# Output projection of the hyena group for all tokens at once, with twice-used weights split once and kept on chip

## The chip, the cores and the metric

The kernel runs on one core of a Trainium2 chip. The metric is device time in microseconds (us) of one execution, the median of several runs. Engines are named as in the profile: PE is TensorE (matrix products), PEld its weight loads, DVE VectorE, ACT ScalarE, POOL GpSimd and SP SyncE, which issues the loads from HBM.

## What is computed

One layer of a diffusion trunk with 512 latent tokens and 256 context tokens, model width 1024, all in float32. Cut to what matters here:

```python
# first half-step SwiGLU, then one input projection p_lat = u_lat @ w_in[layer]
y_lat = jnp.concatenate([hyena_mixer(p_lat[..., :hy_end], *hyena_params),                  # 512 channels
                         diff_head_out(o_lat, diff_subln_g[layer], lam_init)], axis=-1)    # 512 channels
h_lat = h_lat + mod_lat[5] * (y_lat @ w_out[layer])
h_lat = ffn_half_step(h_lat, norm_g[layer, 2], mod_lat[6], mod_lat[7], mod_lat[8], *ffn1)  # RMSNorm, then SwiGLU
return rms_norm(h_lat, final_g)
```

`w_out` is 1024 x 1024. Its first 512 rows meet the hyena group's output (group 0 in the kernel), its last 512 rows the output of the four attention heads (group 1).

## The kernel before

Tokens lie along the free dimension, channels along the 128 partitions. Every float32 operand of a product is split into a high part `h` (a cast to fp32r on ACT, line 253) and a low part `l` (a subtraction on DVE or on POOL, line 254). `mm3` then makes three products from one tile of weights and one of tokens: high by high (line 268), high by low (269), low by high (270).

`stream` brings weights: it loads 1 MB from HBM into one of two raw buffers (line 259) and splits it in two pieces of 128x1024, so one call costs two casts on ACT and two subtractions on DVE or POOL. Without `blocks` the pieces go into rings of three high and three low buffers (`r_h`, `r_l`), where a new piece waits until PE has read the one three pieces back.

Work of this part of the kernel is cut into generators, and the string `SCHEDULE` lists which generator goes on by one step at which place. A `g` behind a word gives the subtractions of that step to POOL, a `v` gives POOL's other elementwise work to DVE. The Tile framework then places the instructions on the engines in about that order; a later, ready instruction may be put ahead of an earlier one that it expects to wait. On the chip every engine runs its own list in order.

The words that the change and the prediction touch:

- `s`, `w`, `a` and `n` with a head and a query block or a half: scores (lines 1196 and 1197, softmax 1199 to 1203), weights of the difference (1213 to 1216), attention (transposes at 1228, products, copy at 1240) and the norm of a head (1254 to 1262). Halves 0 and 1 are tokens 0 to 255 (`SEG_A`) and 256 to 511 (`SEG_B`).
- `J` loads and splits the hyena output. `H0` and `H1` multiply it by group 0 of `w_out`, one half of the tokens each (`wo(0, half)`); `W0` and `W1` do so for the attention output and group 1 (`wo(1, half)`). Each has eight steps, one for every 128 output channels: twelve products of 256 columns and one evacuation (`wo_evac`, line 1269) that adds the result to the residual stream. Each of the four streams `w_out` of its group anew, in two calls of `stream`, at its first and its fifth step.
- `N0` and `N1` are the RMSNorm of a half after the projection: squares on ACT (386, 389), their sum on DVE (391), a product with `ones_d` on PE (399), the inverse root (366 to 369), then eight steps of scaling with a split (407 to 413).
- `F` is the first part of the second SwiGLU, for `N_FIRST` = 2 tiles of hidden channels and each half of the tokens: tiles 0 and 1 of half A, then 0 and 1 of half B. Each has 48 products of 256 columns and streams its weights anew. What the schedule leaves of `F` runs in `plain2`, before the rest of the SwiGLU starts.

`N0` needs the evacuations of `H0` and `W0`, and `N1` those of `H1` and `W1`. In the schedule before, `H0` lies among scores, attention and head norms; `W0` follows it; six of the eight steps of `H1` come between `W0` and the end of `N0`'s scaling, the other two shortly after it.

The on-chip buffers of fp32r words lie at hand-chosen places: the stacked queries and keys of head 3 at 14336 to 18432, the split hyena output at 22528 to 26624, both of `F`'s halves in rings, and the three extra weight buffers of the second SwiGLU (`x`) at 27648, 34880 and 35904.

## Time and profile before

| | us |
|---|---|
| three runs, median (lowest, highest) | 1323.02 (1321.09, 1324.64) |
| the profiled execution, time | 1323.46 |
| the profiled execution, span of its instructions | 1321.7 |
| busy in the span: PE | 1240.0 (94%) |
| DVE | 1088.6 (82%) |
| ACT | 571.0 (43%) |
| POOL | 141.6 (11%) |
| DMA | mean 112 GB/s, 147.82 MB |

A product's duration in the trace runs from its issue to the end of its flow through the array, so that neighbours overlap: for the rate of PE one reads the distance of two starts. A bracket at the end of a row gives the time for which the engine was idle before the instruction, and what ended it. PEclk is the granted clock as a share of 2.4 GHz; 0.50 is 1.2 GHz. The projection and what stands around it take the stretch from about 833 to 976 us of the span.

### The profile page before, as it was taken

What the parts mean: (1) busy time and instruction counts of PE and PEld (TensorE: products, weight loads), DVE (VectorE), ACT (ScalarE), POOL (GpSimd) and SP (SyncE); (2) the same over time, 40 slices, a digit from 0 to 9 for tenths busy, and PEclk for the clock granted to TensorE, in tenths of its full rate; (3) what the DMA queues carried; (4) which work ended last, traced back from release to release, by engine and by line L of the source; (5) the groups of instructions that cost most, each with busy time, mean ns of one, the idle gap of its engine ahead of it and who ended that gap; (6) DMA issues with size and microseconds to landing.
All of it is one profiled execution on the core that took longest, in us unless ns stands there. A gap on an engine that the chain in (4) does not pass through costs nothing.

```text
span 1321.7 us, 19654 instructions
## 1 busy us (share of the span) xinstructions
PE 1240.0 (94%) x7722; PEld 1129.2 (85%) x7722; DVE 1088.6 (82%) x1751; ACT 571.0 (43%) x980; POOL 141.6 (11%) x134
## 2 busy tenths in 40 slices
PE   5899899999999999999989999887899999999996
PEld 2479799999998999999878998776787989989895
DVE  6988899999998765678789667888898978879776
ACT  5652334222331432444343457685553534535343
POOL 3640000000000000000225022113110000000001
PEclk9899999999999999999989999999999999999998
DMA  7646304454573221221323112202342222323221
GB/s 278 218 135 220 114 32 134 154 174 159 176 246 120 84 76 64 80 80 65 109 82 112 49 49 70 75 33 96 128 144 80 98 95 96 123 96 102 96 65 64
DMA packets 30828, 147.82 MB, mean 112 GB/s; under 512 B 3536, under 2 KB 3920, under 8 KB 21648
## 3 DMA queue, kind: packets, MB, share of 16 engines
q1 hardware_dynamic: 28880, 140.28, 31.8%
q0 software_dynamic: 1856, 6.29, 1.3%
q8 instruction: 60, 0.98, 0.3%
q14 instruction: 32, 0.26, 0.1%
HBM read 141.32 MB, written 5.24 MB: 111 GB/s over the span
## 4 chain that ended last, share of the span: by engine, by line
PE 69%; DVE 16%; ACT 4%; DMA 3%; POOL 3%; issue 2%; DVEq 0%; ACTq 0%; POOLq 0%; SPq 0%
PE dc L702 19%; PE ab L702 13%; PE dn L269 6%; PE dn L270 6%; PE dn L268 6%; DVE arena_r L254 3%; ACT arena_r L253 1%; DVE arena_f L353 1%; DVE arena_f L391 1%; DMA arena_f<-in_ada 1%; DMA arena_f<-in_wd 1%; PE gu L269 1%; PE gu L270 1%; DVE arena_f L1199 1%; PE gu L268 1%
## 5 line engine op out<-in xcount | busy, mean ns | idle before, releaser
L680 ACT CAST arena_r<-arena_f 128x512 fp32r<-128x512 f32 x340 | 210.1, 622 | 435.5 <-PE dn L269 167.9
L685 DVE TENSOR_TENSOR arena_r<-arena_f,arena_r 128x512 fp32r<-128x512 f32 x340 | 233.3, 692 | 46.4 <-ACT arena_r L680 40.1
L702 PE MATMUL dc<-arena_r 128*128 128x384 f32 (+1 forms) x1272 | 197.6, 309 | 1.6 <-DVE arena_f L728 1.5
L702 PEld LDWEIGHTS dc<-arena_r 128*128 128x128 f32 x1272 | 188.8, 190 | 2.4 <-DVE arena_f L728 2.1
L253 ACT CAST arena_r<-arena_f 128x1024 fp32r<-128x1024 f32 (+3 forms) x159 | 128.8, 829 | 141.4 <-DVE arena_f L1050 29.1
L254 DVE TENSOR_TENSOR arena_r<-arena_f,arena_r 128x1024 fp32r<-128x1024 f32 (+3 forms) x145 | 144.0, 1009 | 26.7 <-ACT arena_r L253 24.5
L702 PE MATMUL ab<-arena_r 128*128 128x384 f32 (+1 forms) x1008 | 159.3, 309 | 3.0 <-DVE arena_f L921 3.0
L702 PEld LDWEIGHTS ab<-arena_r 128*128 128x128 f32 x1008 | 150.9, 190 | 3.7 <-issue 1.8
L269 PE MATMUL dn<-arena_r,arena_r 128*128 128x512 f32 (+1 forms) x420 | 146.1, 348 | 1.3 <-DVE arena_r L254 1.2
L268 PE MATMUL dn<-arena_r,arena_r 128*128 128x512 f32 (+1 forms) x420 | 145.3, 347 | 1.6 <-ACT arena_r L253 1.6
L270 PE MATMUL dn<-arena_r,arena_r 128*128 128x512 f32 (+1 forms) x420 | 145.2, 346 | 0.0
L754 DVE SCALAR_TENSOR_TENSOR arena_f<-dn,hg,arena_f 128x512 f32<-128x512 f32 (+1 forms) x136 | 83.9, 638 | 47.5 <-PE dn L270 46.9
L673 DVE TENSOR_TENSOR arena_f<-arena_f 128x512 f32<-128x512 f32 x144 | 98.7, 687 | 4.3 <-DMA arena_f<-in_wgu 2.7
L268 PEld LDWEIGHTS dn<-arena_r,arena_r 128*128 128x128 f32 x420 | 79.4, 189 | 12.6 <-ACT arena_r L253 2.5
L269 PEld LDWEIGHTS dn<-arena_r,arena_r 128*128 128x128 f32 x420 | 79.5, 189 | 12.3 <-DVE arena_r L254 2.6
L353 DVE SCALAR_TENSOR_TENSOR arena_f<-arena_f,cs 128x1024 f32<-128x1024 f32 x70 | 88.5, 1280 | 1.6 <-DMA arena_f<-in_ada 1.4
L254 POOL TENSOR_TENSOR arena_r<-arena_f,arena_r 128x1024 fp32r<-128x1024 f32 (+1 forms) x14 | 30.9, 2211 | 544.5 <-DVE arena_f L726 444.2
L270 PEld LDWEIGHTS dn<-arena_r,arena_r 128*128 128x128 f32 x420 | 79.4, 189 | 9.7
L702 PE MATMUL dc<-arena_r,arena_r 128*128 128x384 f32 (+1 forms) x456 | 72.5, 310 | 0.0
L702 PEld LDWEIGHTS dc<-arena_r,arena_r 128*128 128x128 f32 x456 | 68.0, 190 | 0.6
L702 PE MATMUL ab<-arena_r,arena_r 128*128 128x384 f32 (+1 forms) x288 | 47.3, 309 | 0.0
L702 PEld LDWEIGHTS ab<-arena_r,arena_r 128*128 128x128 f32 x288 | 43.6, 190 | 0.0
(306 smaller groups left out, 2604.4 us busy)
## 6 DMA issues: line engine op xcount, KB each, us to landing
arena_f<-in_wgu SPq DMA_DIRECT2D x46, 1024.0 KB, 4.9
arena_f<-in_ada SPq DMA_DIRECT2D x62, 512.0 KB, 3.8
arena_f<-in_wd SPq DMA_DIRECT2D x44, 512.0 KB, 3.6
arena_f<-in_win SPq DMA_DIRECT2D x10, 1024.0 KB, 4.8
arena_f<-in_wout SPq DMA_DIRECT2D x8, 1024.0 KB, 4.8
arena_e<-in_ada SPq DMA_DIRECT2D x10, 512.0 KB, 6.4
arena_f<-in_xT SPq DMA_DIRECT2D x2, 1024.0 KB, 7.3
arena_f<-in_dft SPq DMA_DIRECT2D x2, 1024.0 KB, 4.9
```

Of the source, the lines that this page charges most:

```text
L253: S.copy(hi, src)
L254: eng.tensor_tensor(out=lo, in0=src, in1=hi.bitcast(F32), op=ALU.subtract)
L268: T.matmul(out_, lh, rh, start=start, stop=False)
L269: T.matmul(out_, lh, rl, start=False, stop=False)
L270: T.matmul(out_, ll, rh, start=False, stop=stop)
L353: V.scalar_tensor_tensor(out=acc, in0=w, scalar=sc, in1=acc, op0=ALU.mult, op1=ALU.add)
L391: eng.tensor_tensor(out=acc_b.v(n), in0=acc_b.v(n), in1=sq[k % 2].v(n), op=ALU.add)
L673: V.tensor_tensor(out=o, in0=p, in1=q, op=op)
L680: S.copy(slots[i % NS][0][:, :src.shape[1]], src)
L685: V.tensor_tensor(out=l, in0=src, in1=h.bitcast(F32), op=ALU.subtract)
L702: T.matmul(o, w[:, k, :], b[:, k, :], start=j < 4 and k + n == 0, stop=k == 3 and n == 2, skip_group_check=True)
L754: V.scalar_tensor_tensor(out=dst, in0=t, scalar=hg[:, seg[2], idx, d:d + 1], in1=dst, op0=ALU.mult, op1=ALU.add)
```

## The change

Three places where weights were loaded and split twice are changed.

- `H0` and `H1` become one part `H`, which multiplies the hyena output for all 512 tokens: eight steps of twelve products of 512 columns and one evacuation of 512 columns. Group 0 of `w_out` is streamed in two calls where there were four. In the schedule all steps of `H` stand before `W0`: two among the scores of heads 2 and 3 where four of `H0` stood, and six between `w23` and the second step of `s33`.
- `W0` streams group 1 of `w_out` into eight blocks of its own (`KEEP_AT`), and `W1` reads them again: two calls where there were four. The first four blocks lie where the stacked queries and keys of head 3 are, the other four where the split hyena output is.
- `F` streams its two tiles into eight blocks of its own (`FIRST_AT`) for half A and reads them again for half B: two calls where there were four.

The extra weight buffers `x` of the second SwiGLU move to three of the kept blocks. The words of the schedule other than `H`, `H0` and `H1` keep their order and their suffixes.

```diff
+KEEP = 2
+KEEP_AT = (14336, 15360, 16384, 17408, 22528, 23552, 24576, 25600)
+FIRST_AT = (20480, 21504, 26624, 27648, 32832, 33856, 34880, 35904)
 # SCHEDULE, from the first word that differs (lines wrapped anew)
-Q3g s20 J w20 s21 Q3 K3 a11 H0 a11 s21 w21 a11 K3v s30 s30 s31 H0g s31 a20 a20 w30 H0 a20 s22 H0 s22 w31 a30
-s23 a30 s23 n00g n00 w22 w23 H0 n10 a30 H0g n20g n10g n20 H0 n30 s32 s32 n30 s33 a21 n00g n20 n30g a21 n10 s33
-H0g w32 W0 W0g a21 W0g W0 W0 W0 W0g W0g w33 H1g H1g H1 a31 N0 N0g H1 N0g n01gv a31 a31 N0 H1g H1g N0 n21 N0
-n11 H1 H1g n31 n01 F n21g n11 n31g n31v n01 Fg n11 n21v W1g W1 W1g W1 W1 W1g W1v W1g N1g N1g N1 Fv N1g N1v N1
+Q3g s20 J w20 s21 Q3 K3 a11 H a11 s21 w21 a11 K3v s30 s30 s31 s31 a20 a20 w30 H a20 s22 s22 w31 a30
+s23 a30 s23 n00g n00 w22 w23 H n10 a30 n20g n10g n20 H n30 s32 H s32 H n30 H s33 H a21 n00g n20 n30g a21 n10 s33
+w32 W0 W0g a21 W0g W0 W0 W0 W0g W0g w33 a31 N0 N0g N0g n01gv a31 a31 N0 N0 n21 N0
+n11 n31 n01 F n21g n11 n31g n31v n01 Fg n11 n21v W1g W1 W1g W1 W1 W1g W1v W1g N1g N1g N1 Fv N1g N1v N1
...
     def wo(group, half):
-        seg = (SEG_A, SEG_B)[half]
+        seg = (SEG_A, SEG_B)[half] if group else SEG_L
         if group:
             yh, yl = [b.v(4, 256) for b in yat[half]]
         else:
-            yh, yl = [b.v(4, TL)[:, :, 256 * half:256 * half + 256] for b in late["yhy"]]
+            yh, yl = [b.v(4, TL) for b in late["yhy"]]
         for rw in range(2):
-            res = stream(a["wout"][group, rw])
+            if group:
+                kept = late.setdefault("wkeep", {})
+                if rw not in kept:
+                    blocks = None
+                    if rw < KEEP:
+                        blocks = [R.get(1024, x) for x in KEEP_AT[4 * rw:4 * rw + 4]]
+                        late["wblocks"] = late.get("wblocks", []) + blocks
+                    kept[rw] = stream(a["wout"][group, rw], blocks=blocks)
+                res = kept[rw] if rw < KEEP else kept.pop(rw)
+            else:
+                res = stream(a["wout"][group, rw])
...
-                    t = bank1(f"wo{group}{half}{d}")[:, :256]
+                    t = bank1(f"wo{group}{half}{d}")[:, :seg[1]]
...
     def first_tiles():
+        kept = {}
         for t0, n, _ in (SEG_A, SEG_B):
             for f in range(N_FIRST):
-                wgt = stream(a["wgu"][f])
+                if f not in kept:
+                    blocks = [R.get(1024, x) for x in FIRST_AT[4 * f:4 * f + 4]]
+                    kept[f] = stream(a["wgu"][f], blocks=blocks), blocks
+                wgt = kept[f][0]
...
-               {"x": (A_AT + 9216, R2_AT + 6144, R2_AT + 7168), "act": R2_AT,
+               {"x": (22528, 23552, 24576), "act": R2_AT,
```

## Rows read from the trace of the kernel before

**Rows 1.** The page, part 1 (engine, busy, share, instructions) and part 4 (chain that ended last).

```profile
PE 1240.0 (94%) x7722; PEld 1129.2 (85%) x7722; DVE 1088.6 (82%) x1751; ACT 571.0 (43%) x980; POOL 141.6 (11%) x134
...
PE 69%; DVE 16%; ACT 4%; DMA 3%; POOL 3%; issue 2%; DVEq 0%; ACTq 0%; POOLq 0%; SPq 0%
```

**Rows 2.** Busy time of each engine in six stretches; columns: span, PE, PEld, DVE, ACT, POOL, PEclk, DMA.

```profile
833.00:862.80 29.80, 23.65 (x149) 20.47 (x146) 26.88 (x47) 20.80 (x41) 3.46 (x3) 0.94 0.18 66
862.80:883.50 20.70, 17.82 (x112) 16.02 (x113) 17.06 (x39) 17.26 (x30) 3.62 (x4) 0.92 0.14 44
883.50:898.20 14.70, 14.26 (x114) 13.62 (x113) 13.14 (x22) 10.98 (x23) 3.76 (x3) 1.00 0.25 83
898.20:935.70 37.50, 26.91 (x190) 24.68 (x188) 30.84 (x54) 20.13 (x35) 15.70 (x11) 0.95 0.24 85
935.70:947.60 11.90, 11.76 (x92) 11.20 (x92) 10.97 (x21) 6.00 (x12) 0.00 (x0) 1.00 0.52 178
947.60:976.10 28.50, 21.80 (x147) 20.89 (x147) 21.69 (x38) 15.47 (x24) 4.29 (x4) 0.88 0.32 112
```

**Rows 3.** Instructions on the projection's PSUM tiles: duration min/median/max in ns, first and last start.

```profile
L270 PE MATMUL wo<-arena_r x96: 278/283/415, 835.5 to 947.4; 128*128 128x256 f32 x96
...
L1269 DVE SCALAR_TENSOR_TENSOR arena_f<-wo,mod,arena_f x32: 470/479/487, 837.8 to 947.7; 128x256 f32<-128x256 f32 x32
...
L270 PE MATMUL wo<-arena_r,arena_r x32: 277/283/283, 883.8 to 898.1; 128*128 128x256 f32 x32
```

**Rows 4.** PE in order of time: start, duration; consecutive starts of 256- and 512-column products.

```profile
793.26 0.39 PE L269 MATMUL q_ps<-arena_r 128*128 128x512 f32 x1
...
793.49 0.39 PE L270 MATMUL q_ps<-arena_r 128*128 128x512 f32 x1
...
894.99 0.28 PE L268 MATMUL wo<-arena_r,arena_r 128*128 128x256 f32 x1
...
895.11 0.28 PE L269 MATMUL wo<-arena_r,arena_r 128*128 128x256 f32 x1
```

**Rows 5.** Groups of POOL's instructions, 840 to 985 us: count, busy, mean ns, idle before.

```profile
L254 POOL TENSOR_TENSOR arena_r<-arena_f,arena_r 128x1024 fp32r<-128x1024 f32 x6 | 14.8, 2475 | 13.1 <-ACT arena_r L253 13.1
```

**Rows 6.** DVE in order of time, 899 to 934 us: 128x256 operations and one wait.

```profile
899.09 2.41 DVE L391 TENSOR_TENSOR arena_f<-arena_f 128x256 f32<-128x256 f32 x1 [0.48 <-ACT arena_f L389]
...
902.43 0.42 DVE L391 TENSOR_TENSOR arena_f<-arena_f 128x256 f32<-128x256 f32 x1 [0.54 <-ACT arena_f L389]
...
903.80 2.26 DVE L391 TENSOR_TENSOR arena_f<-arena_f 128x256 f32<-128x256 f32 x1 [0.55 <-ACT arena_f L389]
...
911.30 0.48 DVE L1269 SCALAR_TENSOR_TENSOR arena_f<-wo,mod,arena_f 128x256 f32<-128x256 f32 x1 [2.67 <-PE wo L270]
...
927.74 2.63 DVE L254 TENSOR_TENSOR arena_r<-arena_f,arena_r 128x256 fp32r<-128x256 f32 x1
...
933.55 2.13 DVE L254 TENSOR_TENSOR arena_r<-arena_f,arena_r 128x256 fp32r<-128x256 f32 x1 [0.49 <-ACT arena_r L253]
```

**Rows 7.** PE in order of time, 922 to 964 us: waits, with what ended them.

```profile
922.79 0.48 PE L1256 MATMUL om<-arena_f,ones_e 128*128 128x256 f32 x1 [3.38 <-ACT arena_f L1254]
...
935.74 0.38 PE L269 MATMUL wo<-arena_r 128*128 128x256 f32 x1 [1.78 <-DVE arena_r L254]
...
951.32 0.48 PE L399 MATMUL ms_c<-arena_f,ones_d 128*128 128x256 f32 x1 [3.67 <-DVE arena_f L391]
...
963.38 0.39 PE L269 MATMUL gu<-arena_r 128*128 128x256 f32 x1 [1.92 <-POOL arena_r L413]
```

**Rows 8.** PE in two microseconds after a wait: span, busy, granted clock, DMA.

```profile
952.00:954.00 2.00, 2.00 (x12) 0.50 0.00 0
```

**Rows 9.** Last score product on PE; early split of the first W0 weights on ACT and DVE.

```profile
855.53 1.05 ACT L253 CAST arena_r<-arena_f 128x1024 fp32r<-128x1024 f32 x1
...
878.43 1.22 DVE L254 TENSOR_TENSOR arena_r<-arena_f,arena_r 128x1024 fp32r<-128x1024 f32 x1
...
879.23 0.34 PE L1197 MATMUL sc<-arena_r 128*128 128x384 f32 x1
```

25 lines of the change are left out of this document (14 added, 11 removed).

## The prediction

> **What bounds the kernel now.** I read the page first, then the busy time by stage, then the waits, and last single rows of PE, DVE and POOL around the projection. The page calls PE busy for 94% of the span, but PE carries only 69% of the chain that ended last, and DVE 16% [rows 1]. So there are places where PE waits, and the question is whether the change lies in one of them. The stages say that it does. From 833 to 976.1 us PE is busy for 23.65, 17.82, 14.26, 26.91, 11.76 and 21.80 us of six stretches that last 143.1 us together [rows 2]: 26.9 us are empty, and two thirds of that are in two stretches, the one after `W0` (898.2 to 935.7: 10.6 us empty) and the one after `W1` (947.6 to 976.1: 6.7 us). These are the norms `N0` and `N1`, the scaling and the start of `F`. In the first of them DVE is busy for 30.84 of 37.5 us [rows 2]. Within it I looked at what the long waits of PE end on: an operation of a head norm on ACT (3.38 us), a subtraction on DVE (1.78 us); after `W1` the sum of squares on DVE (3.67 us) and a subtraction on POOL (1.92 us) [rows 7]. Here the vector work sets the pace and PE follows it. `W0` and `W1` themselves are bound by PE: 14.26 of 14.7 us and 11.76 of 11.9 us [rows 2].
>
> **PE's own work: -1.1 us, counted in the stretches below.** A product of 256 columns starts 0.12 us after the one before it, one of 512 columns 0.23 us [rows 4]. The three lines of `mm3` make 3 x (96 + 32) = 384 products for the four old parts [rows 3], that is 96 for each. `H0` and `H1` cost 192 x 0.12 = 23.0 us; `H` costs 96 x 0.23 = 22.1 us. Fewer products are thus no gain by themselves. The evacuations stay about equal: 16 of 0.479 us [rows 3] become 8 that I bound by twice that.
>
> **What moves.** Half of the old work, `H1`, stood after `W0`: 96 x 0.12 = 11.5 us of PE. It now stands ahead of `W0`. I sum by stretch.
>
> *833 to 862.8, no change.* Four old steps (4 x 12 x 0.12 = 5.8 us) give way to two new ones (2 x 12 x 0.23 = 5.5 us).
>
> *862.8 to 883.5, +6.9 us.* Four old steps (5.8 us) give way to six new ones (72 x 0.23 = 16.6 us): 10.8 us more on PE. The stretch has 20.7 - 17.82 = 2.9 us without PE work, and its granted clock is 0.92 [rows 2], so about 0.08 x 20.7 = 1.7 us of full speed are lost. New products can fill at most these 4.6 us, at least nothing: +6.2 to +10.8 us. Because the waits of attention on its splits are scattered and the Tile framework puts ready products into them, I take the idle time whole and half of the lost clock: 10.8 - 2.9 - 0.8 = 7.1, less 0.2 us for evacuations that no longer stand between. DVE (17.06 of 20.7 us) and ACT (17.26) get no new splits here [rows 2], and in a longer stretch they are less full.
>
> *883.5 to 898.2 (`W0`), +1 us.* Twelve products for each of eight steps remain. But the first kept weights lie on the stacked queries and keys of head 3, so their split has to wait for the last score product. Before, the first of these casts ran at 855.53, the second piece was done at 879.65, and the last score product began at 879.23 [rows 9]. Now cast (1.05 us) and subtraction (1.22 us) [rows 9] come behind that product: 2.3 us for the first piece, as much again for the second. On ACT the cast is ahead of attention's copies, on DVE the subtraction ahead of the last head norm. What covers it is the eighth step of `H` (12 x 0.23 = 2.8 us) and the end of attention for head 2; if these have run out, it costs up to 4.5 us, otherwise nothing. I take 1, nearer to the cover, since that step is placed just ahead of those scores. The second four kept blocks lie on the split hyena output and wait for `H` alone, which is past.
>
> *898.2 to 935.7, -14.2 us.* `H1` is gone from here with its 11.5 us of PE and its 8 evacuations (3.8 us of DVE [rows 3]). The four subtractions of `H1` and the two of `W1`'s first weights on POOL are gone, six of 2.475 us [rows 5]. While these run, a 128x256 operation of DVE that takes 0.42 us takes 2.41, 2.26, 2.63 and 2.13 us [rows 6], each about as long as one of POOL's subtractions. That is 9.43 - 4 x 0.42 = 7.75 us of DVE. So of 30.84 us of DVE work 19.3 remain. DVE's idle time here is 6.7 us, and 2.67 of it is an evacuation of `H1` that stands ahead of the inverse root in DVE's queue [rows 6]. With it gone, 4.0 us of waits stay: 19.3 + 4.0 = 23.3 us in place of 37.5. PE has 26.91 - 11.5 = 15.4 us of work left, ACT at most 20.13 [rows 2], both under that. Next late is `W1`, on the head norms' splits, as now. The ends: 18.2 us gain if no wait is left; 6.5 us if `W1` hangs on a chain of ACT and DVE that loses only the 2.67 us wait and the two slow sums (1.99 + 1.84 us).
>
> *935.7 to 947.6 (`W1`), no change.* PE-bound, with its weights now ready.
>
> *947.6 to 976.1, -2 us.* The two tiles of `F` for half B need no load and no split: four casts and four subtractions less (4 x 1.22 us of DVE out of 21.69 [rows 2, 9]), between the scaling steps that PE follows. The wait of 1.92 us [rows 7] is what I count; the sum of squares (3.67 us) stays. Ends: 0 and -4.9 us.
>
> *After 976.1, nothing.* The moved `x` buffers lie on `W1`'s second four kept blocks, which PE has read by 947.6; they are first filled in the SwiGLU after the plain tiles. No queue holds a new wait for them; if the cover were gone, it would be one cast of the eight that run ahead.
>
> Six loads of 1 MB fall away from SP's queue; that is time for DMA, which nothing on the long waits named above was waiting for.
>
> Sum: 6.9 + 1 - 14.2 - 2 = -8.3 us. The profiled execution took 1323.46 us (its span is 1321.7 us, 1.8 us lie outside), 0.44 us over the median of the runs. 1323.46 - 8.3 = 1315.2; against the median 1314.7. I say 1315.
>
> **The rivals.**
>
> *The removed work was hidden (1321 us).* For it: PE is busy for 94% of the span [rows 1], and ACT and POOL have room. Then only PE's 1.1 us and one of DVE's slowed operations count: 1323 - 2. Against it: in the stretch after `W0` DVE is at 82% and PE at 72% [rows 2].
>
> *The fill is gone where it was needed (1328 us, slower).* `H1` was the one large piece of PE work without ties to the norms. In the stretch after `W0` the chain evacuation, square, sum, root, scaling, split remains, and PE then waits more there. The gain is the lower end, 6.5 us, nothing after `W1`, while the stretch before `W0` pays all of its 10.8 us and the late split costs 1 us: 1323 + 10.8 + 1 - 6.5 = 1328. It decides from the point where the gain after `W0` is under the price before it, 7 to 11 us. For it: the head norms' chain on ACT already ended the longest wait there [rows 7]. Against it: DVE's 7.75 us of slowed operations lie on that same stretch.
>
> *The clock (1318 us).* After the wait of 3.67 us ahead of `ms_c` the granted clock is 0.50, that is 1.2 GHz, for the whole of 952 to 954 [rows 7, 8]. With `H1` gone PE has 15.4 us of work in 23.3 us. If the second half of the first tile of `F` (24 products) ran at 0.24 us instead of 0.12, that is 2.9 us, and a few products of `W1` add 0.4 us: 1315 + 3.3. The Trainium skill has a rule that speaks against the change in this way (TensorE: Matmul & The Clock Gate, "HAM oscillation — how this bites in real kernels"): when matmuls come in bursts with waits between them, each burst starts at the low clock again. By that rule the time is this rival's; the trace agrees for the wait of 3.67 us, while after the 3.38 us ahead of a head norm no such row is shown here.
>
> *All of it fits (1305 us).* The idle time before `W0` takes 4.6 us of the new work, the late split costs nothing, the stretch after `W0` gains its whole 18.2 us and the last one 4.9 us: 1323 + 6.2 - 18.2 - 4.9 = 1306; with PE warm before `W0`, 1305.
>
> **How the numbers follow.** Forecast 0.45 (1309 to 1319 by its own ends), clock 0.12, all fits 0.13, hidden 0.15, slower 0.15. The time is the forecast's, 1315. The range goes from the large gain to the hidden case and halfway to the slower one: 1304 to 1325. A difference of 0.3%, about 4 us, is what a measurement of this kernel can tell from none. Faster by more than that: most of the forecast, most of the clock case and all of the large gain, 0.68. Within it: the hidden case, a little of the others, 0.18. Slower: 0.14.
>
> **What would show it.** Right: in the changed trace no subtraction of 128x1024 on POOL between 840 and 985 us and no DVE operation of 128x256 over 2 us there; `W0` ends on PE 6 to 9 us later than 898.2; from there to the first product of `W1` about 23 us; `W1` to the end of `F` 26 to 27 us. Wrong: a stretch after `W0` of more than 30 us, or PE waits of several us ahead of `W0` that end on the split of its weights, or a stretch of scores that grows by more than 11 us because transposes and scores queue behind `H` on PE.

## The result and the profile after

The changed kernel takes 1306.93 us (median of four runs, 1302.81 to 1309.32), the kernel before beside it 1322.29 us (1321.09 to 1324.64): a ratio of 0.9878 with a 95% interval of 0.9849 to 0.9907. The forecast was 1315 with a range of 1304 to 1325. The sign and the range hold, but the forecast gain of 8.3 us is about half of the measured one, 15.4 us between the medians and 16.7 us between the two profiled executions (1323.46 and 1306.77 us).

Line numbers up to that of the projection are three higher in the changed kernel: its cast stands at line 256, the subtraction at 257, the three products of `mm3` at 271 to 273.

The page of the kernel after, busy time by engine and the chain that ended last. Against [rows 1] PE is busy for 7.9 us less, DVE for 17.3 and POOL for 15.1, while PE's share of the chain rises from 69% to 72% and DVE's falls from 16% to 14%: vector work is a smaller part of what sets the end.

```profile
PE 1232.1 (94%) x7626; PEld 1121.4 (86%) x7626; DVE 1071.3 (82%) x1737; ACT 561.1 (43%) x968; POOL 126.5 (10%) x128
...
PE 72%; DVE 14%; ACT 4%; POOL 3%; DMA 3%; issue 2%; DVEq 0%; ACTq 0%; POOLq 0%; SPq 0%
```

The kernel after, busy time of each engine in five stretches (columns as in [rows 2]): the stretch up to the end of attention's scores, `W0`, from the end of `W0` to the first product of `W1`, `W1`, and from there to the first product of the next tile of the SwiGLU.

```profile
830.80:887.60 56.80, 49.18 (x255) 40.69 (x254) 49.61 (x89) 42.80 (x77) 7.86 (x9) 0.97 0.10 35
887.60:903.40 15.80, 15.80 (x120) 15.63 (x119) 11.35 (x22) 8.83 (x18) 0.00 (x0) 0.89 0.44 143
903.40:929.40 26.00, 15.24 (x90) 13.31 (x89) 21.62 (x47) 16.22 (x29) 4.94 (x6) 0.80 0.20 75
929.40:941.10 11.70, 11.70 (x98) 11.50 (x96) 10.03 (x22) 5.57 (x12) 0.00 (x0) 1.00 0.42 137
941.10:960.80 19.70, 18.07 (x148) 17.81 (x148) 18.12 (x36) 10.73 (x20) 2.84 (x4) 1.00 0.09 28
```

Read the spans against the last four rows of [rows 2]: `W0` took 14.7 us and takes 15.8, at a clock of 0.89 where it had 1.00; `W0` to `W1` took 37.5 us and takes 26.0, `W1` took 11.9 and takes 11.7, and the last stretch took 28.5 and takes 19.7. In the last one PE was busy for 21.80 us at a clock of 0.88 in 28.5 us; now it is for 18.07 us at 1.00 in 19.7.

The kernel after, PE in order of time, single rows: the wait ahead of `W0`, the first product after `W0` (a transpose), the longest wait in the stretch after it, the first product of `W1`, the norm's product after `W1`, and the first product of the next tile (`g`).

```profile
887.03 0.39 PE L271 MATMUL o_ps<-arena_r 128*128 128x256 f32 x1 [2.12 <-ACT arena_r L256]
...
903.40 0.38 PE L1231 MATMUL tr<-ident,arena_f 128*128 128x128 f32 x2
...
920.35 2.08 PE L1259 MATMUL om<-arena_f,ones_e 128*128 128x256 f32 x4 [7.20 <-ACT arena_f L1257]
...
929.43 0.28 PE L271 MATMUL wo<-arena_r 128*128 128x256 f32 x1
...
942.65 0.70 PE L402 MATMUL ms_c<-arena_f,ones_d 128*128 128x256 f32 x2 [1.54 <-DVE arena_f L394]
...
960.79 0.40 PE L271 MATMUL g<-arena_r 128*128 128x512 f32 x1
```

One new thing stands out: a wait of 7.20 us for an operation of a head norm on ACT, about twice as long as the longest of [rows 7]. The products of `F` are queued behind it. One old thing is gone: the wait of 3.67 us ahead of `ms_c` is down to 1.54 us.

The kernel after, POOL's groups from 840 to 985 us, all of them (count, busy, mean ns, idle before).

```profile
L1264 POOL TENSOR_SCALAR arena_f<-arena_f,prm 128x256 f32<-128x256 f32 x6 | 3.9, 649 | 47.1 <-DVE arena_f L1263 47.1
L415 POOL TENSOR_SCALAR arena_f<-arena_f,mod 128x256 f32<-128x256 f32 x4 | 3.8, 944 | 51.0 <-ACT arena_r L411 51.0
L416 POOL TENSOR_TENSOR arena_r<-arena_f,arena_r 128x256 fp32r<-128x256 f32 x4 | 3.1, 766 | 0.3
L257 POOL TENSOR_TENSOR arena_r<-arena_f,arena_r 128x256 fp32r<-128x256 f32 x2 | 1.5, 740 | 1.4 <-ACT arena_r L256 1.4
```

The six subtractions of [rows 5] are gone. So are the slowed operations of [rows 6]: over the same 145 us, DVE's sums (L394) and its 128x256 subtractions (L257) have means of 0.42 us.

```profile
L394 DVE TENSOR_TENSOR arena_f<-arena_f 128x256 f32<-128x256 f32 x14 | 5.9, 421 | 1.3 <-ACT arena_f L392 1.1
...
L257 DVE TENSOR_TENSOR arena_r<-arena_f,arena_r 128x256 fp32r<-128x256 f32 x6 | 2.5, 420 | 0.0
```

### The profile page after: what moved, and what is told of

Read it like the earlier page. It is cut to its first block, busy times and chain, and to the rows that moved or that the text cites. A ratio compares the mean times of both kernels' runs of the same rounds, so it can differ in the third digit from the quotient of the medians.

```text
span 1305.0 us, 19391 instructions
## 1 busy us (share of the span) xinstructions
PE 1232.1 (94%) x7626; PEld 1121.4 (86%) x7626; DVE 1071.3 (82%) x1737; ACT 561.1 (43%) x968; POOL 126.5 (10%) x128
## 4 chain that ended last, share of the span: by engine, by line
PE 72%; DVE 14%; ACT 4%; POOL 3%; DMA 3%; issue 2%; DVEq 0%; ACTq 0%; POOLq 0%; SPq 0%
PE dc L705 19%; PE ab L705 14%; PE dn L272 6%; PE dn L273 6%; PE dn L271 6%; DVE arena_r L257 3%; DMA arena_f<-in_ada 1%; ACT arena_r L256 1%; DVE arena_f L356 1%; DMA arena_f<-in_wd 1%; PE gu L272 1%; PE wo L271 1%; PE wo L272 1%; PE wo L273 1%; PE gu L271 1%
## 5 line engine op out<-in xcount | busy, mean ns | idle before, releaser
L705 PE MATMUL dc<-arena_r 128*128 128x256 f32 (+1 forms) x1500 | 226.2, 306 | 0.2 <-DVE arena_f L731 0.2
L705 PEld LDWEIGHTS dc<-arena_r 128*128 128x128 f32 x1500 | 216.7, 190 | 1.5 <-DVE arena_f L731 0.6
L705 PE MATMUL ab<-arena_r 128*128 128x256 f32 (+1 forms) x1152 | 176.9, 306 | 3.1 <-DVE arena_f L924 3.1
L705 PEld LDWEIGHTS ab<-arena_r 128*128 128x128 f32 x1152 | 168.2, 190 | 3.8 <-issue 1.9
L272 PE MATMUL dn<-arena_r,arena_r 128*128 128x512 f32 (+1 forms) x448 | 156.2, 349 | 1.3 <-DVE arena_r L257 1.2
L271 PE MATMUL dn<-arena_r,arena_r 128*128 128x512 f32 (+1 forms) x448 | 155.0, 348 | 1.6 <-ACT arena_r L256 1.6
L257 DVE TENSOR_TENSOR arena_r<-arena_f,arena_r 128x1024 fp32r<-128x1024 f32 (+3 forms) x139 | 132.6, 969 | 27.8 <-ACT arena_r L256 25.6
L273 PE MATMUL dn<-arena_r,arena_r 128*128 128x512 f32 (+1 forms) x448 | 155.3, 347 | 0.0
L272 PEld LDWEIGHTS dn<-arena_r,arena_r 128*128 128x128 f32 x448 | 84.9, 190 | 12.9 <-DVE arena_r L257 2.6
L271 PEld LDWEIGHTS dn<-arena_r,arena_r 128*128 128x128 f32 x448 | 84.6, 190 | 13.2 <-ACT arena_r L256 2.5
L273 PEld LDWEIGHTS dn<-arena_r,arena_r 128*128 128x128 f32 x448 | 84.8, 189 | 10.5
L257 POOL TENSOR_TENSOR arena_r<-arena_f,arena_r 128x1024 fp32r<-128x1024 f32 (+1 forms) x8 | 16.1, 2013 | 531.9 <-DVE arena_f L729 444.4
L705 PE MATMUL dc<-arena_r,arena_r 128*128 128x384 f32 x228 | 42.6, 336 | 0.0
L705 PEld LDWEIGHTS dc<-arena_r,arena_r 128*128 128x128 f32 x228 | 39.4, 188 | 0.2
L737 DVE TENSOR_TENSOR arena_f<-dc,arena_f 128x768 f32<-128x768 f32 (+1 forms) x36 | 29.6, 823 | 9.6 <-PE dc L705 9.5
```

The source lines that it names most:

```text
L257: eng.tensor_tensor(out=lo, in0=src, in1=hi.bitcast(F32), op=ALU.subtract)
L271: T.matmul(out_, lh, rh, start=start, stop=False)
L272: T.matmul(out_, lh, rl, start=False, stop=False)
L273: T.matmul(out_, ll, rh, start=False, stop=stop)
L705: T.matmul(o, w[:, k, :], b[:, k, :], start=j < 4 and k + n == 0, stop=k == 3 and n == 2, skip_group_check=True)
L737: V.tensor_tensor(out=o, in0=dc.rearrange("p (b w) -> p b w", b=2)[:, :, :HT], in1=st["u"].unsqueeze(1).to_broadcast([P, 2, HT]), op=ALU.add)
```

## The experiments

Each kernel was timed beside the kernel before on the same chip, and the ratio is to that; a gain in us below is one minus the ratio, times the median of that kernel before (1322.29 to 1325.67 us). For the stages I use marks on PE that every kernel has: the last product on `kc_ps` (the keys of head 3, the last work ahead of the touched stretch), the product `ms_c` of `N0`, the last product of `W1`, the first product `g` of the next SwiGLU tile (in `e2_f_resplit`, where three of them come 11.7 us earlier, the first behind the last product of `F`), and the first product `ab` (the start of the long even part of that SwiGLU). Distances in us, one trace each:

| kernel | gain by times | kc to N0 | N0 to end of W1 | W1 to g | kc to ab | ab to end |
|---|---|---|---|---|---|---|
| before | | 74.2 | 40.5 | 28.8 | 166.8 | 322.2 |
| after | 16.1 | 75.6 | 34.7 | 20.0 | 153.8 | 320.7 |
| after_again | 15.4 | 75.7 | 34.9 | 20.0 | 154.1 | 320.7 |
| e1_f_rings | 14.6 | 75.6 | 32.3 | 25.2 | 156.5 | 320.4 |
| e2_f_resplit | 15.0 | 75.5 | 32.9 | 24.3 | 155.5 | 320.5 |
| e3_w_rings | 14.1 | 76.9 | 35.8 | 22.5 | 158.7 | 320.7 |
| e4_f_alone | 4.6 | 75.2 | 42.5 | 23.6 | 164.7 | 323.3 |
| h_alone | 3.8 | 77.8 | 35.1 | 28.4 | 164.7 | 319.9 |
| h_moved | 3.0 | 76.8 | 34.7 | 29.2 | 164.1 | 323.0 |
| w_alone | 4.1 | 75.3 | 40.9 | 24.1 | 163.8 | 320.9 |
| before_dve | 5.8 | 70.5 | 37.8 | 29.9 | 161.6 | 321.8 |
| e5_swap | 14.2 | 76.5 | 34.1 | 20.5 | 154.6 | 320.9 |
| e6_norms | 16.8 | 76.2 | 32.2 | 21.9 | 153.8 | 320.8 |
| f_early | 15.6 | 76.4 | 33.9 | 20.5 | 154.3 | 321.3 |

The last column is work that no kernel here changes but for the place of the `x` buffers, and it still differs by up to 3.4 us from trace to trace. The start of the touched stretch does so too: the last `kc_ps` product begins between 829.7 and 834.9 us in these traces, with the same instructions ahead of it. A difference of that size between two single profiles is thus no effect; the distances inside the touched stretch are the better evidence (the same kernel twice, after and after_again: 153.8 and 154.1).

**The kernel after, again.** The same kernel once more, so that its times and its stages can be set against the parts below.

> The changed kernel itself once more, beside the three that follow, so that they are compared on one chip: ratio to the kernel before 0.985 to 0.990.

1307.72 us against 1324.93, ratio 0.9884 (0.9848 to 0.9919). The stages agree with the first trace within 0.3 us.

### Where the gain after `W1` came from

**F through the rings.** `H` and the kept `W` weights stay; each half of `F` loads and splits its tiles anew.

```diff
-                if f not in kept:
-                    blocks = [R.get(1024, x) for x in FIRST_AT[4 * f:4 * f + 4]]
-                    kept[f] = stream(a["wgu"][f], blocks=blocks), blocks
-                wgt = kept[f][0]
+                wgt = stream(a["wgu"][f])
```

> The changed kernel, but F streams and splits its weights for each half again, through the rings as before; H and the kept weights of W0 and W1 stay. The two traces put 8.8 us of the gain into the stretch after W1 (28.5 us before, 19.7 us after), where 2 us were forecast. If F's kept weights are the cause of it, this kernel is 6 to 9 us slower than the changed one, about 1314, and its stretch after W1 is back at 26 to 28 us, with casts on ACT that wait for PE to leave a ring buffer. Rival: the stretch shrank because H1 and the subtractions on POOL are gone and W1 starts earlier; then this kernel is within 3 us of the changed one.

1310.44 us, ratio 0.9890 (0.9863 to 0.9918). The stage after `W1` becomes 5.2 us longer (25.2 for 20.0), a little less than expected, and the whole is only 2.7 us longer from `kc_ps` to `ab`, and by the times it can't be told from the whole change. What was missed: the stage ahead of it becomes 2.4 us shorter (32.3 for 34.7). In the kernel after, where `F` has blocks of its own, the split of its second tile and the first split of the tile behind it come early, amid `N0`'s scaling. The kernel after, DVE in order of time, from the inverse root of `N0` to its last scaling steps:

```profile
909.28 0.43 DVE L372 SCALAR_TENSOR_TENSOR arena_f<-arena_f 128x256 f32<-128x256 f32 x1
909.62 1.22 DVE L257 TENSOR_TENSOR arena_r<-arena_f,arena_r 128x1024 fp32r<-128x1024 f32 x1
910.75 0.87 DVE L410 SCALAR_TENSOR_TENSOR arena_f<-arena_f,gsc 128x256 f32<-128x256 f32 x2
...
912.54 1.22 DVE L257 TENSOR_TENSOR arena_r<-arena_f,arena_r 128x1024 fp32r<-128x1024 f32 x1
...
919.36 1.22 DVE L257 TENSOR_TENSOR arena_r<-arena_f,arena_r 128x1024 fp32r<-128x1024 f32 x1
920.49 0.88 DVE L413 SCALAR_TENSOR_TENSOR arena_r<-arena_f,mod,arena_r 128x256 fp32r<-128x256 f32 x2
```

With the rings full, that can't be: DVE of the kernel with `F` through the rings has one subtraction ahead of the scaling and the next one behind it, and the scaling between them (914.75 to 922.38) isn't broken:

```profile
904.68 1.22 DVE L257 TENSOR_TENSOR arena_r<-arena_f,arena_r 128x1024 fp32r<-128x1024 f32 x1
...
914.75 1.26 DVE L410 SCALAR_TENSOR_TENSOR arena_f<-arena_f,gsc 128x256 f32<-128x256 f32 x3
...
922.38 0.48 DVE L413 SCALAR_TENSOR_TENSOR arena_r<-arena_f,mod,arena_r 128x256 fp32r<-128x256 f32 x1
...
929.77 1.23 DVE L257 TENSOR_TENSOR arena_r<-arena_f,arena_r 128x1024 fp32r<-128x1024 f32 x1 [0.15 <-ACT arena_r L256]
```

So part of what leaves the stage after `W1` is paid in the stage before it.

**F split again into its own blocks.** This takes the rings away and leaves the loads, casts and subtractions.

```diff
                 if f not in kept:
-                    blocks = [R.get(1024, x) for x in FIRST_AT[4 * f:4 * f + 4]]
-                    kept[f] = stream(a["wgu"][f], blocks=blocks), blocks
-                wgt = kept[f][0]
+                    kept[f] = None, [R.get(1024, x) for x in FIRST_AT[4 * f:4 * f + 4]]
+                wgt = stream(a["wgu"][f], blocks=kept[f][1])
```

> The changed kernel, but F loads and splits its two tiles for half B again, into the same own blocks as for half A. The work of the four casts and four subtractions is back, the wait for a ring buffer is not (the first tile's block has long been read; the second's is free when PE is through with half A's second tile). If the waits in ACT's queue make the gain, this is within 3 us of the changed kernel, 1307 to 1310. If the work itself does (4 x 1.05 us of ACT, 4 x 1.22 us of DVE between the scaling steps), it is as slow as the kernel with rings, about 1314.

1309.50 us, ratio 0.9887 (0.9861 to 0.9914). After `W1` it takes 24.3 us: of the 5.2 us only 0.9 go with the rings, 4.3 stay. So a second split costs, whichever buffer it goes to. The trace of this kernel after `W1`, DVE and ACT in order of time:

```profile
951.79 1.75 DVE L257 TENSOR_TENSOR arena_r<-arena_f,arena_r 128x1024 fp32r<-128x1024 f32 x1
...
956.18 1.21 DVE L257 TENSOR_TENSOR arena_r<-arena_f,arena_r 128x1024 fp32r<-128x1024 f32 x1
...
946.36 1.05 ACT L256 CAST arena_r<-arena_f 128x1024 fp32r<-128x1024 f32 x1 [3.71 <-PE gu L272]
...
947.84 1.31 ACT L411 ACTIVATE arena_r<-arena_f,mod 128x256 fp32r<-128x256 f32 x3
```

The cast still waits for PE, 3.71 us, which I had not expected: half A's products of the second tile read the block that it is to fill, and the scaling steps of `N1` (L411) stand behind it in ACT's queue; the subtractions stand between scaling steps on DVE. What the work of the second split costs and what this wait costs is thus not told apart.

**W through the rings.** `H` and the kept `F` stay; `W0` and `W1` each load and split.

```diff
-            if group:
-                kept = late.setdefault("wkeep", {})
...
-                res = kept[rw] if rw < KEEP else kept.pop(rw)
-            else:
-                res = stream(a["wout"][group, rw])
+            res = stream(a["wout"][group, rw])
```

> The changed kernel, but W0 and W1 stream group 1 through the rings, each for itself; H and F's kept weights stay. W0's weights can be split before the last scores again, so the 2.12 us that PE waits ahead of W0 should go; W1's four casts and four subtractions come back, two of them on POOL, between W0 and W1. Theory of the sum: -2 us ahead of W0, +4 to +6 us ahead of W1 (two 128x256 operations of DVE slowed by 1.9 us each, two subtractions of 1.22 us): 1309 to 1312. Rival: the stretch ahead of W1 is set by the waits of PE on the head norms' squares, and the splits are hidden; then 1304 to 1306.

1311.27 us, ratio 0.9894 (0.9872 to 0.9916). The time is in the range that I had given, but not by its terms: the wait ahead of attention's products, which was to go, is 2.54 us for 2.12, and the stage up to `N0` becomes 1.3 us longer, not 2 us shorter. From `kc_ps` to `ab` it is 4.9 us longer than the kernel after, of which 2.5 after `W1`. There PE waits twice as long for the sums of `N1` (first row; the kernel after had 1.54 us), and among these sums stand the two subtractions of the tile behind `F`: they begin at 943.06 and 944.93, in the kernel after at 919.36 and 928.07. With `F` through the rings, and `W` kept, the wait is 1.54 us as in the kernel after (second row, from that kernel). PE in the two kernels:

```profile
946.54 0.70 PE L402 MATMUL ms_c<-arena_f,ones_d 128*128 128x256 f32 x2 [3.06 <-DVE arena_f L394]
...
944.57 0.70 PE L402 MATMUL ms_c<-arena_f,ones_d 128*128 128x256 f32 x2 [1.54 <-DVE arena_f L394]
```

**F alone.** The kernel before with the kept blocks of `F` and the moved `x` buffers.

```diff
+FIRST_AT = (20480, 21504, 26624, 27648, 32832, 33856, 34880, 35904)
...
-                wgt = stream(a["wgu"][f])
+                if f not in kept:
+                    blocks = [R.get(1024, x) for x in FIRST_AT[4 * f:4 * f + 4]]
+                    kept[f] = stream(a["wgu"][f], blocks=blocks), blocks
+                wgt = kept[f][0]
```

> The kernel before with F's kept weights alone (and the extra weight buffers of the second SwiGLU moved as in the change); H0, H1, W0 and W1 as before. If F's part of the gain stands by itself, this kernel gains 6 to 9 us on the kernel before: 1313 to 1316, with the stretch after W1 at about 20 us. If it needs the rest of the change, the gain is 0 to 3 us.

1320.23 us, ratio 0.9965 (0.9950 to 0.9979): 4.6 us faster, less than expected. After `W1` it gains 5.2 us (23.6 for 28.8), as in the first experiment, and it gives 2.0 us back between `N0` and the end of `W1` (42.5 for 40.5), as there. By its trace the gain from `kc_ps` to `ab` is 2.1 us, by the times 4.6; that difference stays open.

### The parts by themselves

**H alone.** The changed kernel with the two ring edits above: only the merged part `H` in its new place (the `x` buffers stay moved).

```diff
-                wgt = kept[f][0]
+                wgt = stream(a["wgu"][f])
...
-                res = kept[rw] if rw < KEEP else kept.pop(rw)
+            res = stream(a["wout"][group, rw])
```

> H for all tokens with the schedule of the change, but W0, W1 and F load and split for each half through the rings. From kc_ps (the last key product of the context) to the first group of the second SwiGLU the changed kernel takes 153.8 us, 13.0 less than before; leaving out F's kept weights adds 2.7, leaving out W's adds 4.9. If the three parts add up, H alone gains 5 to 6 us: about 1316 to 1318 where the kernel before takes 1323. If they cover each other (the splits are only hidden as long as H1 is gone or the other way round), H alone gains either nothing (0 to 2) or nearly all (9 to 12).

1319.69 us, ratio 0.9971 (0.9951 to 0.9991). That lies between the cases that I had set, 5 to 6 us and 0 to 2, and decides for neither. It pays before `N0` (+3.6 us) and gains between `N0` and the end of `W1` (-5.4), as the sum of the change had it; the net is small.

**The old `H0` and `H1` in the new places.** The code before, with the schedule of after in which each of the first four `H` is `H0 H0` and each of the last four `H1 H1`.

```diff
-s20 J w20 s21 Q3 K3 a11 H0 a11 s21 w21 a11 ...
+s20 J w20 s21 Q3 K3 a11 H0 H0 a11 s21 w21 a11 ...
...
-a30 s23 n00g n00 w22 w23 H0 n10 a30 H0g n20g n10g n20 H0 n30 s32 s32 n30 s33 a21 ...
+a30 s23 n00g n00 w22 w23 H0 H0 n10 a30 n20g n10g n20 H0 H0 n30 s32 H1 H1 s32 H1 H1 n30 H1 H1 s33 H1 H1 a21 ...
```

> The kernel before with the schedule of the change: H0 and H1 stay two parts with their own loads, splits and 256-column products, but all sixteen of their steps stand ahead of W0, two at each place of a step of H. It differs from H alone (0.9971 of the kernel before, 3.8 us) by the merging only: four casts and four subtractions more ahead of W0, and 0.9 us more of PE. If the gain of H alone comes from merging, this kernel is 3 to 5 us slower than H alone, that is equal to the kernel before or slower by 1 to 2 us. If it comes from the new place (nothing between W0 and the norm any more, no subtractions on POOL beside the sum of squares), it is within 1.5 us of H alone.

1321.54 us, ratio 0.9977 (0.9957 to 0.9996), beside 0.9971 for `H`; from `kc_ps` to `ab` 164.1 and 164.7 us. Merging the halves, which saves two loads and four splits, brings nothing that can be told here. What `H` does in this kernel, its place and its missing `g` do, as far as these times can tell.

**W alone.** The kernel before with `W0`'s weights kept for `W1`.

```diff
+KEEP = 2
+KEEP_AT = (14336, 15360, 16384, 17408, 20480, 21504, 26624, 27648)
...
-            res = stream(a["wout"][group, rw])
+            if group:
+                kept = late.setdefault("wkeep", {})
...
+                    kept[rw] = stream(a["wout"][group, rw], blocks=blocks)
+                res = kept[rw]
```

> The kernel before with W's kept weights alone (blocks at free places); H0, H1 and F as before. F alone gained 4.7 us (ratio 0.9965), H alone 3.8 (0.9971), H with W's 14 to 15 (0.989), H with F's 14 (0.9894), all three 15.5 (0.9884). If each kept set gains about 10 us only where H is whole and stands ahead of W0, W alone gains 0 to 5 us. If W's kept weights gain by themselves what they gain beside H, it gains 8 to 10 us, and then the parts do not need each other.

1318.92 us, ratio 0.9969 (0.9952 to 0.9985). Its whole gain in the touched stretch is after `W1` (24.1 for 28.8), where I had counted nothing for it.

So alone the parts give 3.8, 4.6 and 4.1 us, 12.5 together; all three give 15 to 16. Two with `H` give 14 to 15, and the third set of kept weights adds some 1 to 2 us by the times, less than they resolve (2.7 and 4.9 us by the traces).

### POOL

**The six subtractions on DVE.** The kernel before without the change; three `g` are dropped from its schedule, so that DVE and not POOL does the subtractions of [rows 5].

```diff
-w33 H1g H1g H1 a31 N0 N0g H1 N0g n01gv a31 a31 N0 H1g H1g N0
+w33 H1 H1g H1 a31 N0 N0g H1 N0g n01gv a31 a31 N0 H1 H1g N0
...
-W1g W1 W1g W1 W1 W1g W1v W1g
+W1 W1 W1g W1 W1 W1g W1v W1g
```

> The kernel before, with the six subtractions of 128x1024 that ran on POOL (four of H1, two of W1's first weights) given to DVE. DVE gets 6 x 1.22 = 7.3 us of work, and four 128x256 operations fall from 2.1 to 2.6 us back to 0.42 (7.75 us), one more ahead of them by 2.2 us. If POOL's subtractions cost DVE what the sum says, the kernel is between 3 us faster and equal. Rival: they were work that DVE was spared, and the slowed operations lay on no path; then it is 4 to 7 us slower.

1317.40 us, ratio 0.9956 (0.9938 to 0.9974): 5.8 us faster, more than expected. DVE of this kernel in order of time, three of the sums of `N0`:

```profile
890.89 0.41 DVE L391 TENSOR_TENSOR arena_f<-arena_f 128x256 f32<-128x256 f32 x1
...
892.98 0.41 DVE L391 TENSOR_TENSOR arena_f<-arena_f 128x256 f32<-128x256 f32 x1
...
895.86 0.42 DVE L391 TENSOR_TENSOR arena_f<-arena_f 128x256 f32<-128x256 f32 x1
```

Two of the seven sums of `N0` took 2.41 and 2.26 us in [rows 6] beside POOL's subtractions, and the first of the seven, at 893.99, took 2.63: 6.0 us more than the three need. DVE gets four of the six subtractions in the stage up to `N0`, 4.9 us. The stage is 3.7 us shorter, more than the 1.1 us that are left of this, and the one up to the end of `W1` 2.7 us; where the rest comes from isn't shown. DVE has six more operations of 1.22 us to do and the kernel is faster. About a third of what the change brings is thus to be had by three letters in the schedule, without any kept weights.

### The two new waits

**The kept blocks exchanged.** The first four blocks of `W0` and of `F` change places, so that `W0`'s first weights need not wait for the last scores.

```diff
-KEEP_AT = (14336, 15360, 16384, 17408, 22528, 23552, 24576, 25600)
-FIRST_AT = (20480, 21504, 26624, 27648, 32832, 33856, 34880, 35904)
+KEEP_AT = (20480, 21504, 26624, 27648, 22528, 23552, 24576, 25600)
+FIRST_AT = (14336, 15360, 16384, 17408, 32832, 33856, 34880, 35904)
```

> The changed kernel with two places exchanged: the first kept weights of W0 lie where F's first tile lay (free early), F's first tile lies on the stacked queries and keys of head 3. Nothing else differs. The split of W0's first weights no longer waits for the last score product. The sum priced that wait at 1 us (0 to 4.5). In the changed trace PE waits 2.12 us ahead of W0, on a copy of attention that stands behind the late cast in ACT's queue. If the late split is the cause, that wait goes and the kernel gains 1 to 3 us; if the wait is attention's own, it stays and the time is within 1 us of the changed kernel.

1309.17 us, ratio 0.9893 (0.9857 to 0.9928), beside 0.9884 for the change: no gain. Its PE, the last score product and the first attention product behind it:

```profile
890.85 0.34 PE L1200 MATMUL sc<-arena_r 128*128 128x384 f32 x1
...
893.32 0.39 PE L271 MATMUL o_ps<-arena_r 128*128 128x256 f32 x1 [2.13 <-ACT arena_r L256]
```

The wait of 2.1 us ahead of attention is the same as in the kernel after. By itself that doesn't clear the late split, for now `F`'s first split is late in its place: a cast of 128x1024 on ACT starts 2.3 us after the last score product in both kernels (893.16 here, 886.87 there). But the kernel with `W` through the rings has no weights on those blocks, and its PE waits there too:

```profile
887.22 0.58 PE L271 MATMUL o_ps<-arena_r 128*128 128x256 f32 x1 [2.54 <-ACT arena_r L256]
```

So the wait doesn't hang on the late split. And the last score product comes 56.4 us after `kc_ps`, where it came 54.1; I read this as the early splits, which stand ahead of softmax in the queues of ACT and DVE. What is moved out of `W0`'s way goes in the way of the scores.

**F's first weights earlier.** The first of `F`'s two loads and splits becomes a step of its own, placed among the scores of head 3.

```diff
+        blocks = [R.get(1024, x) for x in FIRST_AT[:4]]
+        kept = {0: (stream(a["wgu"][0], blocks=blocks), blocks)}
+        yield
         late["act"] = A.get(N_FIRST * TL)
...
-H n30 H s33 H a21
+H F n30 H s33 H a21
```

> The changed kernel with the load and split of F's first tile listed ahead, among the last steps of H, where its blocks are free. In the changed trace both of F's tiles are split between W0 and the scaling of N0 (casts at 908.45 to 913.45 us), in the stretch that DVE limits, and the kernel whose F goes through the rings has W1 start 2.4 us earlier than the changed one. If these splits delay the scaling, moving one tile's two casts and two subtractions (2.1 us of ACT, 2.4 us of DVE) out of there makes the stretch from N0's product to the end of W1 1 to 3 us shorter and the kernel 1 to 3 us faster. Rival: the stretch ahead of W0 is as full, and what is won behind W0 is lost ahead of it; then it is within 1 us of the changed kernel.

1308.74 us, ratio 0.9882 (0.9847 to 0.9917): no difference from the change. The stage up to `N0` is 0.8 us longer, the next 0.8 shorter; the last score product again comes at 56.4 us. The casts from 908.45 to 913.45 that I had named are not those of both tiles of `F`: they belong to its second tile and to the tile behind it, and the first tile was split during `W0` (897.37 to 901.5). Two subtractions still stand amid `N0`'s scaling here (913.12 and 919.93). What is won in one stage is paid in the other.

**The head norms later.** The wait of 7.20 us is taken away: the head norm's products no longer stand ahead of `F`'s on PE.

```diff
-w33 a31 N0 N0g N0g n01gv a31
-a31 N0 N0 n21 N0 n11 n31 n01 F n21g n11 n31g n31v n01 Fg n11 n21v W1g
+w33 n01gv n11 a31 N0 N0g n21 N0g n01 n11 a31
+a31 N0 N0 N0 F n31 n01 n11 n21g n31g n31v Fg n21v W1g
```

> The changed kernel with another order of words between W0 and W1: the norms of heads 0 and 1 of the second half start ahead of N0, and F's first tile is listed ahead of the norm of head 3. In the changed trace PE stands 7.20 us ahead of a head norm's product that waits for ACT, with F's products behind it, of which five eighths could run. If that order costs time, the stretch from N0's product to the end of W1 (34.8 us) falls by 3 to 7 us and the kernel gains as much. Rival: DVE, at 15.4 of 20 us there, sets the time, and PE's wait is free; then the gain is under 1.5 us.

1305.85 us, ratio 0.9873 (0.9836 to 0.9910), beside 0.9884: the lowest median, but not to be told from the change. Its PE around the place where the wait was:

```profile
916.88 0.56 PE L271 MATMUL gu<-arena_r 128*128 128x256 f32 x1
...
924.69 1.05 PE L1259 MATMUL om<-arena_f,ones_e 128*128 128x256 f32 x2
```

Its clock from 912 to 926 us (PE alone: span, busy, granted clock, DMA):

```profile
912.00:926.00 14.00, 11.39 (x44) 0.50 0.00 0
```

`F` starts at 916.88, 84.9 us after `kc_ps`; in the kernel after it starts 91.4 us after it. The end of `W1` comes 2.5 us sooner after `N0`, the stage behind it is 1.9 us longer, and from `kc_ps` to `ab` both take 153.8 us. That the wait is gone is thus worth nothing that can be told. Two readings are left, and no run parts them: that DVE's list, which is no shorter, sets the pace, or that the low clock takes back what the wait gave, since from the first product of `F` to the first of `W1` this kernel takes 12.1 us where the kernel after takes 7.57, and the clock behind `W1` is 0.92 and not 1.00.

## Why the prediction was right, and which term was mis-sized

Between the two profiled executions, by the prediction's own stages:

| stretch | forecast, us | measured, us |
|---|---|---|
| ahead of the touched stretch | 0 | 832.74 to 830.51: -2.2 |
| to the end of `W0`, with the late split | +7.9 | 65.5 to 72.9: +7.4 |
| end of `W0` to the first product of `W1` | -14.2 | 37.5 to 26.0: -11.5 |
| `W1` | 0 | 11.6 to 11.4: -0.2 |
| end of `W1` to `g` | -2 | 28.8 to 20.0: -8.8 |
| after that | 0 | 345.6 to 344.2: -1.4 |
| sum | -8.3 | -16.7 |

(`W1` here from its first to its last product.) The first and the last row are of the size by which traces with the same instructions there differ. The touched stretch itself gave 13.1 us, and the medians of the runs 15.4; these 2.3 us, and the spread of the last stage, stay unexplained.

**Ahead of `W0`: right.** +7.4 us against +6.9 and +1. From `kc_ps` to the last score product it is 7.6 us more (46.5 and 54.1): `H` could fill only the few places that were empty, as worked out. From there to the end of `W0` it is 0.1 us less, where I had 1 us for the late split. That includes a cost that I had at nothing: after the wait of 2.12 us the granted clock is 0.50 from 889 to 891 us, and `W0` takes 1.1 us longer.

**After `W0`: right in mechanism, the gain 2.7 us smaller.** PE's work is 15.24 us as forecast (15.4), POOL's subtractions and DVE's slowed operations are gone. DVE does 21.62 us where I said 19.3, the stretch takes 26.0 where I said 23.3, and PE's clock is 0.80. DVE's 2.3 us are about two more subtractions of 1.22 us: four of 128x1024 lie in this stretch now (from 909.62 to 928.07), two did before (912.30 and 923.38). With blocks of their own, weights are split earlier, and some of that work now lies here. Here the clock rival came in in part. The clock in slices of 2 us from 918, after the wait of 7.20 us:

```profile
918.00:920.00 2.00, 0.00 (x0) 0.50 0.03 12
920.00:922.00 2.00, 1.66 (x5) 0.50 0.00 0
922.00:924.00 2.00, 2.00 (x10) 0.50 0.00 0
924.00:926.00 2.00, 2.00 (x13) 0.62 0.00 0
926.00:928.00 2.00, 2.00 (x19) 1.00 0.00 0
```

PE does 10 products in a slice at 0.50 (1.2 GHz) and 19 at 1.00 (2.4 GHz). The first tile of `F`, 48 products, takes 7.57 us instead of 48 x 0.12 = 5.8: 1.8 us, where that rival had 2.9, and `W1` ran at 1.00, where it had 0.4. The Trainium skill (TensorE: Matmul & The Clock Gate, "HAM oscillation — how this bites in real kernels") has each burst start at the low clock again when matmuls come in bursts with waits between them; the trace agrees for this wait. It doesn't for two others: after the 3.38 us of [rows 7] PE does 19 products at 1.00 from 924 to 926 us, and after the 3.06 us with `W` through the rings 19 at 1.00 from 947.5 to 949.5. Whether the 1.8 us cost the kernel anything stays open, for the experiment that takes the wait away has the low clock too. That DVE sets the pace here, as the prediction read it from its 82% in [rows 2], is argued and not shown.

**After `W1`: the mis-sized term.** I took -2 us, with an end at -4.9; it was -8.8, beyond the end that I had set. The step that failed is "the sum of squares (3.67 us) stays", and the choice of the 1.92 us wait as the price; the clock of this stretch, 0.88 [rows 2], had no term at all. I read in [rows 7] that PE waits for the sum of squares and took this for a chain of the norm itself. But what stands among these sums in DVE's queue are the splits of `F`: those of its second tile for half A (the second of them at 945.76) and the first for half B (948.64). The kernel before after `W1`, DVE in order of time, then ACT:

```profile
945.76 1.23 DVE L254 TENSOR_TENSOR arena_r<-arena_f,arena_r 128x1024 fp32r<-128x1024 f32 x1
...
948.64 1.22 DVE L254 TENSOR_TENSOR arena_r<-arena_f,arena_r 128x1024 fp32r<-128x1024 f32 x1
...
949.78 1.48 DVE L391 TENSOR_TENSOR arena_f<-arena_f 128x256 f32<-128x256 f32 x3
...
954.04 1.28 DVE L407 SCALAR_TENSOR_TENSOR arena_f<-arena_f,gsc 128x256 f32<-128x256 f32 x3
...
956.30 1.05 ACT L253 CAST arena_r<-arena_f 128x1024 fp32r<-128x1024 f32 x1 [3.73 <-PE gu L269]
...
957.26 1.31 ACT L408 ACTIVATE arena_r<-arena_f,mod 128x256 fp32r<-128x256 f32 x3
```

Two things are to be seen. The subtraction at 948.64 runs ahead of the last three sums, which end at 951.3, where PE's wait ends. And the scaling on ACT (L408) could have followed L407, which starts at 954.04; it starts at 957.26 because a cast for half B of `F` stands ahead of it in ACT's list and waits 3.73 us for PE to be done with the ring's old block; PE reaches those products late, behind its own wait of 3.67 us. The change takes out more than the four subtractions for half B that I counted: half A's second tile is split before `W1` too (909.62 and 912.54). In the kernel after, the same place, DVE then ACT:

```profile
935.86 1.23 DVE L257 TENSOR_TENSOR arena_r<-arena_f,arena_r 128x1024 fp32r<-128x1024 f32 x1
...
942.17 0.42 DVE L394 TENSOR_TENSOR arena_f<-arena_f 128x256 f32<-128x256 f32 x1
...
945.40 1.28 DVE L410 SCALAR_TENSOR_TENSOR arena_f<-arena_f,gsc 128x256 f32<-128x256 f32 x3
...
945.91 1.31 ACT L411 ACTIVATE arena_r<-arena_f,mod 128x256 fp32r<-128x256 f32 x3 [1.99 <-DVE arena_f L410]
```

From 935.86 to the next tile there is no 128x1024 subtraction, the last sum runs 1.3 us after `W1`'s last product, and ACT's scaling follows DVE's by 0.5 us. PE's waits after `W1` fall from 6.7 to 1.5 us and its clock is 1.00 instead of 0.88. Of the 8.8 us, 5.1 are time without work on PE, and 3.7 are PE's own time for the same products (21.80 and 18.07 us), which is the clock. The waits of PE after `W1` in the traces show which part of the change takes out which, in us:

| weights | kernels | wait ahead of `ms_c` | all later waits |
|---|---|---|---|
| `W` and `F` split twice | before; `h_alone` | 3.67; 3.14 | 3.04; 2.34 |
| `W` kept | `e1_f_rings`; `w_alone` | 1.54; 1.54 | 3.01; 2.43 |
| `F` kept | `e3_w_rings`; `e4_f_alone` | 3.06; 3.99 | 0.76; 0 |
| both kept | after; `after_again` | 1.54; 1.55 | 0; 0 |

So the wait for the sum of squares goes with `W1`'s own splits, and the waits amid the scaling, the 1.92 us with them, go with the second splits of `F`; neither part takes out both. As I read the rows, `W1`'s splits held up those behind them, until they fell among the sums. The experiments divide the 8.8 us: `F` through the rings gives 5.2 of them back, `W` through the rings 2.5, `H` alone gains 0.4. Splitting `F` again into blocks of its own gives 4.3 back; how much of that is work and how much the cast's wait for PE isn't shown.

But the gain of this stage is not the gain of the kernel. The kept `F` costs 2.4 us earlier, where three subtractions of 1.22 us now stand amid `N0`'s scaling, and its net is 2.7 us by the traces. I had priced each stage as if it were apart; the vector work that leaves one of them lets work of another move.

**The rivals.** Hidden (1321) and slower (1328) are out: the touched stretch gained, and the fill was not missed. The time of "all of it fits" (1305) is nearest, but it came another way: the stretch before `W0` was not as cheap, the one after `W0` gained 11.5 and not 18.2 us, and the stage after `W1` gave more than its upper end. That the clock falls after a long wait held, at 1.8 of its 3.3 us. The measured 1306.93 lies under the forecast's own ends, 1309 to 1319: the range holds it because it was drawn down to the large gain, not because the sum was right. Two small sums were off as well, without effect on the range: PE's own work is 0.96 us less (192 x 0.12 against 96 x 0.23), not 1.1, and the hidden case, this and one slowed operation of some 1.9 us, comes to 1320.

**The signs that I named.** No 128x1024 subtraction on POOL and no 128x256 operation of DVE over 2 us: so it is. `W0` 6 to 9 us later: 5.2 us by the absolute time, 7.4 us from `kc_ps`. About 23 us from there to `W1`: 26.0. `W1` to the end of `F` 26 to 27: 20.0, the miss told above. None of the signs of being wrong came: the stretch after `W0` is under 30 us, the wait ahead of `W0` is 2.12 us, and the scores come 7.6 us later, not 11.

**What stays open.** Why two parts with `H` give more than their sum (14.6 and 14.1 us where 7.9 and 8.4 would be the sums), though after `W1` the table shows two waits that need two parts; whether the gain of `H` is its place or its four subtractions that POOL no longer does, since no kernel had the new place with POOL's subtractions; whether DVE's list or the clock sets the pace after `W0`; and the differences between times and traces or sums named above (`F` alone, the change's 2.3 us, the six subtractions on DVE).

## What to carry to other kernels

When a wait ends on a short operation of a norm, read what stands ahead of that operation in its engine's list before calling the wait the norm's own: here it was weight splits that belonged to the next stage, held up by those of the stage before, and a cast that waited for a buffer held up a scaling that was ready. Weights that two halves use are best split once where vector work sets the pace, but a stage's gain is not the kernel's, since DVE's list takes in the next work, and in two trials moving the same splits earlier only paid them elsewhere. Where a wait on PE goes, count the clock with it: 3.7 of the 8.8 us after `W1` were the same products at the higher clock. Ask of work given to an idle engine what it does to the busy one beside it; here a trial of three letters would have shown a third of the gain.

## What the runs showed of the hardware

That POOL's subtractions slow DVE was in [rows 6]; that leaving all of them to a DVE that is already at 82% of the stretch makes the kernel 5.8 us faster was not expected. Each takes 2475 ns on POOL [rows 5] and 1.22 us on DVE, and while POOL had one, a sum of 0.42 us took up to 2.41 us. The Trainium skill (SBUF — State Buffer, "SBUF: two separate sides") has DVE operations with two on-chip inputs and operations of GpSimd exclude each other, each for the whole instruction; the rows agree, in that the slowed operations last about as long as one subtraction of POOL.

The other thing is the spread inside the trace: with the same instructions ahead of it, the start of the touched stretch differs by up to 5.1 us (829.7 to 834.9 us), so that a change of 3 us can't be read from the ends of two traces, but from distances between marks inside the touched stretch.
